# A hybrid decoder layer: the gate's row through DRAM, shift columns in the high operand alone, and the mean square of both boundaries with tokens on partitions

## The chip, the cores and the metric

The kernel runs on one core of one Trainium2 chip. The metric is the time on the device in microseconds (us), the median over timed runs. PE is TensorE's matmul stream, PEld its weight loads, DVE VectorE, ACT ScalarE, POOL GpSimd, SP the engine that issues the weight transfers.

## The reference

One decoder layer on 256 tokens of 1024 features, all in float32: a conditioning vector gives nine modulation rows; then a SwiGLU block (ffn1), a mixer of a state-space branch (SSD) and a retention branch, a second SwiGLU block (ffn2), and a last norm.

```python
def rms_normalize(x):
    return x * rsqrt(mean(x * x, axis=-1, keepdims=True) + EPS)
def modulate(x, shift, scale):
    return x * (1.0 + scale) + shift
def swiglu(x, w_in, w_out):
    gate, up = split(x @ w_in, 2, axis=-1)
    return (silu(gate) * up) @ w_out

mod = silu(c) @ ada_w + ada_b
sh1, sc1, g1, sh2, sc2, g2, sh3, sc3, g3 = split(mod, 9, axis=-1)
u = modulate(rms_normalize(h) * norm_ffn1_w, sh1, sc1)
h = h + 0.5 * g1 * swiglu(u, ffn1_w_in, ffn1_w_out)
u = modulate(rms_normalize(h) * norm_mix_w, sh2, sc2)
h = h + g2 * hybrid_mixer(u, ...)      # u @ mix_w_in, conv, SSD, retention, gates, mix_w_out
u = modulate(rms_normalize(h) * norm_ffn2_w, sh3, sc3)
h = h + 0.5 * g3 * swiglu(u, ffn2_w_in, ffn2_w_out)
return rms_normalize(h) * norm_final_w
```

## The kernel before

Activations lie transposed: features on the 128 partitions (eight tiles of 128 features, "kt" when they are contracted), the 256 tokens along the free axis. Weights come once from DRAM in tiles of 1 MB, issued on SP into four buffers (`wst`). Each tile is split in two halves, and each half in a high part (ACT, L137) and a low part (DVE, L138) of type fp32r, into four buffers `wh`; activations have a high and a low part too (`uh`, `ul`). Each product is three matmuls (mm3): high weights with `uh` (L152), high weights with `ul` (L153), low weights with `uh` (L154), 256 columns each; every fifth kt has the same three in another order (L148 to L150). Products of fp32 operands, a handful, are made by PE in several passes; the trace counts each pass.

There are two boundaries, the end of ffn1 and the end of the mixer. There `contract` finishes h feature tile by feature tile; `done` (in `residual`) scales it, adds its square to a running sum, and writes h·am, not normalised, to `ha` and `uh`/`ul`. `modulated` then runs the first four tiles of the next projection early, on this unnormalised h·am (`early_project`), because the scale 1/rms of a token can be applied to the products afterwards. The modulation's shift must not be scaled by it, so it rides along as two more columns: the moving operand is 258 columns wide, and column 256 of the product becomes a bias (`eb`). The first tiles take four PSUM banks. At kt = 1 (first boundary) or kt = 2 (second), `rstd` is called: two fp32 matmuls with a 128x128 matrix of 1/1024 sum the squares over the features and spread the result to all partitions (L223), ACT takes a logarithm and an exponential, and DVE corrects the result in four instructions (L228 to L231). `rs`, 128x256, then multiplies h·am (L274), from which the proper u is made for all later tiles (L240, L241), and the four early products (L281). `rstd` is used inside the mixer too, for its norms.

The mixer's steps run in the order of the string `ORDER`. A scheduler places each step's instructions on the engines within that order. The step "dt" projects 32 columns, turns them with an fp32 matmul (L613) and makes dt and `av` on DVE (L616 to L631); "z.0.0" is the first gate tile; "decays" makes three groups of fp32 matmuls on `av` (L684, L687, L692); "conv" steps project two tiles and run a convolution of four taps on ACT and DVE (L574, L577).

In ffn2's loop, at p2 == 5, the row 0.5·g3 (1024 values that lie on the partitions as 128x8) is made into `gb`, the same row on all 128 partitions: a diagonal matrix on DVE (L992), two fp32 matmuls with a matrix of ones (L996) and two copies on ACT (L998). `gb` is first read at the end of ffn2 (L1014), where tokens lie on the partitions.

Of the kernel before, what the change touches and what calls it, by code (L numbers as in the profile page):

```python
# [12 lines left out]
F32 = mybir.dt.float32  # L13
# [3 lines left out]
ALU = mybir.AluOpType  # L17

P = 128
# [19 lines left out]
U_ROW = 320  # L39
HALVES_AT = {"still": (6, 1056), "alike": (48, 1072)}  # L40

K_TRI, K_M = 0, 128
K_INV, K_SGN = 256, 257
N_CONST = 258

H_ID, H_N1, H_AB = KD * T, KD * T + P, KD * T + P + KD
N_HEAD = H_AB + 2 * KD
# [5 lines left out]
F1 = 8  # L53

ORDER = (
# [12 lines left out]
def constants():  # L68
    c = np.zeros((P, N_CONST), np.float32)
    i = np.arange(P)  # L70
    c[:, K_TRI:K_TRI + P] = i[:, None] <= i[None, :]
    c[:, K_M:K_M + P] = 1.0 / D
    c[:, K_INV] = 10000.0 ** (-(i % 64) / 64.0)
    c[:, K_SGN] = np.where(i < 64, -1.0, 1.0)
    lg = np.log1p(-np.exp2(-5.0 - np.arange(8)))
    rel = np.arange(T)[None, :] - i[:, None]
    dm = np.where(rel >= 0, np.exp(lg[:, None, None] * np.maximum(rel, 0)), 0.0) * P ** -0.5
    dm = np.ascontiguousarray(dm.transpose(1, 0, 2).reshape(P, 8 * T)).astype(np.float32)
    return c, dm
# [3 lines left out]
def layer(ctx: ExitStack, tc: tile.TileContext, a, out, packing):  # L83
# [72 lines left out]
    def at(pair, *idx):  # L156
        return pair[0][idx], pair[1][idx]

    def wide_at(u, kt):
        return u[2][:, kt, :], u[3][:, kt, :]  # L160

    al = slice(None)

# [2 lines left out]
    h = head[:, :KD * T].rearrange("p (f t) -> p f t", f=KD)  # L166
    ident = head[:, H_ID:H_ID + P]
    triu = k[:, K_TRI:K_TRI + P]
    mean_m = k[:, K_M:K_M + P]
    ones = cst.tile([P, P], F32, name="ones")  # L170
    dve.memset(ones, 1.0)
    epsc = cst.tile([P, 1], F32, name="epsc")
    dve.memset(epsc, EPS)

# [45 lines left out]
    def rstd(parts, mean):  # L220
        ps = misc_ps()
        for i, s in enumerate(parts):
            pe.matmul(ps[:, :T], mean, s, start=i == 0, stop=i == len(parts) - 1)  # L223
        rs = sp.tile([P, T], F32, tag="rs", name=nm("rs"), bufs=2)
        t = sp.tile([P, T], F32, tag="rt", name=nm("rt"), bufs=2)
        lookup(rs, ps[:, :T], AF.Ln, bias=epsc)
        lookup(rs, rs, AF.Exp, scale=-0.5)
        dve.tensor_tensor(t, rs, rs, ALU.mult)  # L228
        dve.scalar_tensor_tensor(t, ps[:, :T], EPS, t, ALU.add, ALU.mult)
        dve.tensor_scalar(t, t, -0.5, 1.5, ALU.mult, ALU.add)  # L230
        dve.tensor_tensor(rs, rs, t, ALU.mult)  # L231
        return rs

    def new_u():
        full = [sp.tile([P, KD, U_ROW], F32R, tag=n, name=nm(n), bufs=1) for n in ("uh", "ul")]
        return tuple(t[:, :, :T] for t in full) + tuple(t[:, :, :T + 2] for t in full)

    def u_tile(u, f, t, jsh):
        sh = modc[:, jsh, f:f + 1]
        act.activation(u[0][:, f, :], t, AF.Identity, bias=sh)  # L240
        dve.scalar_tensor_tensor(u[1][:, f, :], t, sh, u[0][:, f, :].bitcast(F32),  # L241
                                 ALU.add, ALU.subtract)
# [20 lines left out]
    ready = []  # L263

    def modulated(ha, u, jsh, w, cols, at_kt=1, c_next=None):
        rs = []
        ps = early_project(w, cols, u, at_kt, lambda: rs.append(rstd(sums, mean_m)))
        rs = rs[0]
        if c_next is not None:
            st = load(w, 0, KD, c_next, 256)  # L270
            ready.append(half(st[:, :, :P]))
        for f in range(KD):
            t = ha(f)
            dve.tensor_tensor(t, t, rs, ALU.mult)  # L274
            u_tile(u, f, t, jsh)
        if c_next is not None:
            ready.append(half(st[:, :, P:]))
        b = sp.tile([P, 4], F32, tag="eb", name=nm("eb"), bufs=1)
        for i in range(4):
            dve.tensor_copy(b[:, i:i + 1], ps[i][:, T:T + 1])  # L280
            dve.tensor_tensor(ps[i][:, :T], ps[i][:, :T], rs, ALU.mult)  # L281
        return [(ps[i][:, :T], b[:, i:i + 1]) for i in range(4)]

    def early_project(w, cols, u, at_kt, between):
        sts = [load(w, 0, KD, c0, 256) for c0 in cols]
        ps = [proj_ps().rearrange("p f t -> p (f t)") for _ in range(2)]
        ps += [misc_ps() for _ in range(2)]
        for kh in range(2):
            hv = [half(st[:, 4 * kh:4 * kh + 4, :]) for st in sts]
            for kk in range(4):  # L290
                kt = 4 * kh + kk
                if kt == at_kt:
                    between()
                for i in range(2):
                    for f in range(2):
                        mm3(ps[2 * i + f][:, :T + 2], at(hv[i], al, kk, slice(f * P, (f + 1) * P)),
                            wide_at(u, kt), kt == 0, kt == KD - 1)
        return ps

    def pair_halves(w, c0):  # L300
# [20 lines left out]
    def residual(jg, factor, am, ha, u, jsh):  # L321
        g = sp.tile([P, KD], F32, tag="g", name=nm("g"), bufs=2)
        dve.tensor_scalar(g, modc[:, jg, :], factor, None, ALU.mult)

        def shift():
            split_into(u[2][:, :, T:], u[3][:, :, T:],
                       modc[:, jsh, :].unsqueeze(2).broadcast_to([P, KD, 2]))

        def done(f, ps):
            if f == KD - 2:  # L330
                shift()
            dve.scalar_tensor_tensor(h[:, f, :], ps, g[:, f:f + 1], h[:, f, :], ALU.mult, ALU.add)
            square_add(f)
            act.activation(ha(f), h[:, f, :], AF.Copy, scale=am[:, f:f + 1])
            act.activation(u[0][:, f, :], h[:, f, :], AF.Copy, scale=am[:, f:f + 1])
            dve.tensor_tensor(u[1][:, f, :], ha(f), u[0][:, f, :].bitcast(F32), ALU.subtract)
        return done
# [17 lines left out]
    with (tc.tile_pool(name="ep", bufs=1) as ep,  # L355
# [25 lines left out]
        for kt in range(3):  # L381
            sts.append(ada01(kt))
            wst.append(w01(kt))
        mean1 = ep.tile([P, 1], F32, name="mean1")
        dve.memset(mean1, 1.0 / D)
        bn1 = ep.tile([P, KD], F32, name="bn1")
        cps, stat = [misc_ps() for _ in range(2)], misc_ps()
        for q in range(2):
# [107 lines left out]
    with tc.tile_pool(name=nm("fp"), bufs=1, reuse_waits="tile") as fp:  # L496
# [11 lines left out]
        for p2 in range(4, NF // 2):  # L508
# [5 lines left out]
            if p2 == 8:  # L514
# [21 lines left out]
                    dve.tensor_scalar(rr, rr, pi_lo, -pi_lo, ALU.min, ALU.max)  # L536
                    lookup(dst, rr, AF.Sin)
                dve.tensor_scalar(rope_s, rope_s, k[:, K_SGN:K_SGN + 1], None, ALU.mult)
        table("natural_log_exp_and_others")
        while ada_todo[0][0] in (2, 4):  # L540
            ada_next()
        am = scale_col(V_N2, 4)
# [4 lines left out]
    with tc.tile_pool(name="mx", bufs=1, reuse_waits="tile") as mx:  # L547
# [19 lines left out]
        def conv_pair(f0, dst):  # L567
            ps = pair_project(w_in, C_XS + f0 * P, u)
            t = mx.tile([P, 2, T], F32, tag="cv", name=nm("cv"), bufs=2)
            for f in range(2):  # L570
# [5 lines left out]
                for sh in (1, 2, 3):  # L576
# [3 lines left out]

        table_of = {"e": "natural_log_exp_and_others", "s": "silu_and_others",
                    "g": "sigmoid_and_others"}
        now = ["e"]

        def need(t):
            if now[0] != t:
# [366 lines left out]
        phase["uses"].append(cast)  # L953
        while ada_todo[0][0] == 7:
            ada_next()
        table("natural_log_exp_and_others")
        am = scale_col(V_N3, 7)
        hA = [slot([P, 4, T]) for _ in range(2)]

# [7 lines left out]
    with tc.tile_pool(name=nm("fp"), bufs=1, reuse_waits="tile") as fp:  # L967
# [5 lines left out]
        for p2 in range(NF // 2):  # L973
            if p2 == 0:
                s = fp.tile([P, 2, T], F32, tag="s", name=nm("s"), bufs=2)
                for f in range(2):
                    lookup(s[:, f, :], first[f][0], AF.Silu, bias=first[f][1])
                    dve.scalar_tensor_tensor(s[:, f, :], first[2 + f][0], first[2 + f][1],
                                             s[:, f, :], ALU.add, ALU.mult)
                split_into(ah[:, 0:2, :], alo[:, 0:2, :], s)  # L980
            else:
                pg = pair_project(w1, p2 * 256, u, ready if p2 == 1 else None)
                pu = pair_project(w1, FFN + p2 * 256, u)
                swiglu(fp, pg, pu, ah, alo, 2 * p2)
            ada_next()
            if p2 == 1:
                nc.sync.dma_start(wf, a["norm_final_w"].broadcast_to([P, D]))
            if p2 == 5:
                g = sp.tile([P, KD], F32, tag="g", name=nm("g"), bufs=2)
                dve.tensor_scalar(g, modc[:, 8, :], 0.5, None, ALU.mult)  # L990
                diag = fp.tile([P, KD, P], F32, tag="diag", name="diag")
                dve.tensor_tensor(diag, ident.unsqueeze(1).broadcast_to([P, KD, P]),  # L992
                                  g.unsqueeze(2).broadcast_to([P, KD, P]), ALU.mult)
                for q in range(2):
                    ps = misc_ps()
                    pe.matmul(ps, ones, diag[:, 4 * q:4 * q + 4, :].rearrange("p f t -> p (f t)"),  # L996
                              start=True, stop=True)
                    act.copy(gb[:, q * 512:(q + 1) * 512], ps)  # L998
            if p2 == 6:
                for tt in range(2):  # L1000
                    for q in range(2):
                        ps = misc_ps()
                        for f in range(4):
                            pe.transpose(ps[:, f * P:(f + 1) * P],
                                         h[:, q * 4 + f, tt * P:(tt + 1) * P], ident)
                        act.copy(hN[:, tt, q * 512:(q + 1) * 512], ps)
# [105 lines left out]
```

## Time and profile before

| | |
|---|---|
| median of 3 runs | 830.82 us (829.90 to 831.51) |
| profiled execution | 830.36 us, its span 828.3 us |
| granted TensorE clock, mean | 0.998 |
| PE busy | 816.0 us, 6610 instructions |
| DVE busy | 664.9 us, 997 instructions |
| ACT busy | 511.8 us, 731 instructions |
| POOL busy | 10.3 us, 21 instructions |

A row of a timeline has the start and the duration in us, the engine, the line, the operation, output<-inputs, the shapes and a count of instructions taken together; a bracket tells how long the engine stood idle before and what released it. A row of waits has the total in us, the number of times and the longest. A row of stretches has the bounds and the length, then busy us and (instructions) of PE, PEld, DVE, ACT and POOL, the granted clock, the DMA share and GB/s. Rows by form end in busy us and mean ns of one. Rows of the chain have start, duration and what held it.

### The profile page before, as it was taken

How to read it: one execution, taken by the hardware profiler on the slowest of the kernel's cores; microseconds unless marked ns; L12 is line 12 of the kernel's file. 1: busy time of each engine (PE TensorE's matmuls, PEld its weight loads, DVE VectorE, ACT ScalarE, POOL GpSimd, SP SyncE). 2: the span in 40 equal slices, each digit the busy share in tenths (PEclk: the TensorE clock that was granted, in tenths of full speed). 3: DMA queues.
4: the chain of work that ended last, by engine and by line, in shares of the span. 5: the costliest groups of instructions: out<-in, count | busy, mean ns of one | idle time of the engine just before them, and what ended most of it. 6: DMA issues, size and time to landing. Idle time of an engine off the chain costs nothing.

```text
span 828.3 us, 15880 instructions
## 1 busy us (share of the span) xinstructions
PE 816.0 (99%) x6610; PEld 786.7 (95%) x6610; DVE 664.9 (80%) x997; ACT 511.8 (62%) x731; POOL 10.3 (1%) x21
## 2 busy tenths in 40 slices
PE   8999999999999999999999999999999999999996
PEld 6999999999999989999999999999999999999885
DVE  6999899977989987787898778977979985455463
ACT  6565455555898787766465569765568654545442
POOL 0000000000200010000000000000000000000000
PEclk9999999999999999999999999999999999999999
DMA  9998899854695465537658754555665695455521
GB/s 361 413 419 333 317 365 350 344 180 161 238 316 190 167 216 181 196 133 237 233 184 301 253 205 153 209 199 173 219 215 183 256 345 197 169 196 183 206 77 51
DMA packets 30297, 193.06 MB, mean 233 GB/s; under 512 B 3457, under 2 KB 4097, under 8 KB 9618
## 3 DMA queue, kind: packets, MB, share of 16 engines
q1 hardware_dynamic: 28512, 186.59, 62.1%
q0 software_dynamic: 1568, 5.28, 2.0%
q8 instruction: 51, 0.84, 0.4%
q10 hardware_dynamic: 146, 0.20, 0.1%
q14 instruction: 20, 0.16, 0.1%
HBM read 190.97 MB, written 1.08 MB: 232 GB/s over the span
## 4 chain that ended last, share of the span: by engine, by line
PE 88%; DVE 4%; ACT 3%; DMA 3%; issue 1%; SPq 0%; ACTq 0%
PE proj L154 22%; PE proj L152 22%; PE proj L153 22%; PE proj L1028 7%; PE proj L148 2%; PE proj L149 2%; PE proj L150 2%; DMA wst<-in_ffn_w_in_dram 2%; ACT wh L407 1%; DMA ada<-in_ada_w_dram 1%; PE misc L757 1%; DVE wh L138 1%; PE misc L901 1%; DVE wh L410 1%; DVE ada L197 1%
## 5 line engine op out<-in xcount | busy, mean ns | idle before, releaser
L138 DVE TENSOR_TENSOR wh<-wst,wh 128x1024 fp32r<-128x1024 f32 (+1 forms) x262 | 316.7, 1212 | 110.5 <-ACT wh L137 109.8
L137 ACT CAST wh<-wst 128x1024 fp32r<-128x1024 f32 (+1 forms) x262 | 272.3, 1042 | 174.6 <-PE proj L154 104.0
L152 PE MATMUL proj<-uh,wh 128*128 128x256 f32 (+1 forms) x1144 | 317.9, 278 | 0.0
L153 PE MATMUL proj<-ul,wh 128*128 128x256 f32 (+1 forms) x1144 | 316.8, 277 | 0.5 <-DVE ul L429 0.5
L154 PE MATMUL proj<-uh,wh 128*128 128x256 f32 (+1 forms) x1144 | 316.6, 277 | 0.2 <-DVE wh L410 0.2
L153 PEld LDWEIGHTS proj<-ul,wh 128*128 128x128 f32 x1144 | 214.8, 188 | 1.2 <-DVE ul L429 0.7
L154 PEld LDWEIGHTS proj<-uh,wh 128*128 128x128 f32 x1144 | 214.8, 188 | 0.6 <-DVE wh L410 0.4
L152 PEld LDWEIGHTS proj<-uh,wh 128*128 128x128 f32 x1144 | 214.9, 188 | 0.3 <-ACT wh L137 0.2
L152 PE MATMUL proj<-s,wh 128*128 128x256 f32 x312 | 87.1, 280 | 0.2 <-ACT s L142 0.2
L154 PE MATMUL proj<-s,wh 128*128 128x256 f32 x312 | 86.4, 277 | 0.0
L153 PE MATMUL proj<-s,wh 128*128 128x256 f32 x312 | 86.2, 277 | 0.0
L152 PEld LDWEIGHTS proj<-s,wh 128*128 128x128 f32 x312 | 58.5, 188 | 0.6 <-ACT s L142 0.4
L153 PEld LDWEIGHTS proj<-s,wh 128*128 128x128 f32 x312 | 58.6, 188 | 0.2 <-issue 0.2
L154 PEld LDWEIGHTS proj<-s,wh 128*128 128x128 f32 x312 | 58.6, 188 | 0.0
L197 DVE SCALAR_TENSOR_TENSOR ada<-ada,cb 128x1024 f32<-128x1024 f32 x48 | 57.4, 1217 | 0.0
L1028 PE MATMUL proj<-wh,ah 128*128 128x512 f32 (+1 forms) x188 | 55.0, 376 | 0.5 <-DVE t L1014 0.5
L148 PE MATMUL proj<-uh,wh 128*128 128x256 f32 x152 | 42.0, 277 | 0.0
L149 PE MATMUL proj<-uh,wh 128*128 128x256 f32 x152 | 42.0, 276 | 0.0
L150 PE MATMUL proj<-ul,wh 128*128 128x256 f32 x152 | 42.0, 276 | 0.0
L153 PE MATMUL proj<-al,wh 128*128 128x256 f32 x152 | 42.0, 276 | 0.0
L152 PE MATMUL proj<-ah,wh 128*128 128x256 f32 x152 | 42.0, 276 | 0.0
L154 PE MATMUL proj<-ah,wh 128*128 128x256 f32 x152 | 42.0, 276 | 0.0
(276 smaller groups left out, 1303.2 us busy)
## 6 DMA issues: line engine op xcount, KB each, us to landing
wst<-in_mix_w_in_dram SPq DMA_DIRECT2D x52, 1024.0 KB, 4.9
wst<-in_ffn_w_in_dram SPq DMA_DIRECT2D x43, 1024.0 KB, 6.4
wst<-in_ffn_w_out_dram SPq DMA_DIRECT2D x18, 1024.0 KB, 5.1
ada<-in_ada_w_dram SPq DMA_DIRECT2D x16, 1024.0 KB, 8.4
wst<-in_ada_w_dram SPq DMA_DIRECT2D x12, 1024.0 KB, 5.0
ada<-in_ada_w_dram SPq DMA_DIRECT2D x16, 512.0 KB, 12.7
wst<-in_w_br_ssd_dram SPq DMA_DIRECT2D x8, 1024.0 KB, 4.9
wst<-in_w_br_ret_dram SPq DMA_DIRECT2D x8, 1024.0 KB, 4.9
```

The costliest lines, as they stand in the source:

```text
L137: act.copy(hi, v)
L138: dve.tensor_tensor(lo, v, hi.bitcast(F32), ALU.subtract)
L148: pe.matmul(o, l[1], r[0], start=False, stop=False, skip_group_check=skip)
L149: pe.matmul(o, l[0], r[0], start=False, stop=False, skip_group_check=skip)
L150: pe.matmul(o, l[0], r[1], start=False, stop=False, skip_group_check=skip)
L152: pe.matmul(o, l[0], r[0], start=first, stop=False, skip_group_check=skip)
L153: pe.matmul(o, l[0], r[1], start=False, stop=False, skip_group_check=skip)
L154: pe.matmul(o, l[1], r[0], start=False, stop=last, skip_group_check=skip)
L197: dve.scalar_tensor_tensor(st[:, i, :], st[:, i, :], 1.0, cb, ALU.mult, ALU.mult, accum_out=raw[:, j, f0 + i:f0 + i + 1])
L407: act.copy(hw[0][j], wst[kt][:, j, :])
L410: dve.tensor_tensor(hw[1][j], wst[kt][:, j, :], hw[0][j].bitcast(F32), ALU.subtract)
L1028: pe.matmul(ps[tt][:, part], l[:, kt, ts], r, start=kt == n == 0, stop=n == 2 and kt == NF - 1, skip_group_check=bi == 1)
```

## The change

Four things are changed.

1. The gate's row: the 128x8 tile is written to DRAM in feature order, and read back broadcast to all partitions, by two DMAs on POOL's queue. Diagonal, matmuls and copies are gone.
2. The shift columns: the high part of the shift stands in column 256 of `uh` and its low part in column 257. The middle matmul of an early product takes 256 columns of `ul`; the bias is the sum of both columns of the product (a reduction over two elements in place of a copy). The other two matmuls stay at 258.
3. The mean square at both boundaries: the sums of squares are the stationary operand and a single column of 1/1024 the moving one, two halves of 128 tokens each (`stat`), so that the mean square comes out with tokens on partitions, 128x2. The second `stat`, for the last feature's square, stands behind the first pair of tiles of that kt. A square root on ACT and a reciprocal on DVE follow on 128x2. One pair of tiles after the start of the next kt, two matmuls with r broadcast as stationary operand and the identity as moving one spread r as a 128x256 tile in PSUM (`spread`). The first four features are multiplied straight from PSUM, the others and the four early products by a copy in SBUF (`rs`). The tables loaded on ACT change to suit.
4. `ORDER` begins with "z.0.0 dt" in place of "dt z.0.0". The constant tile `k` is 128 columns narrower, since the mean matrix isn't needed, so all tiles allocated behind it lie 480 bytes lower in each partition (448 for some).

```diff
@@ constants @@
-K_TRI, K_M = 0, 128
-K_INV, K_SGN = 256, 257
-N_CONST = 258
+K_TRI, K_INV, K_SGN = 0, 128, 129
+N_CONST = 130
@@ ORDER @@
-    "dt z.0.0 decays ml.0 ml.1 conv.8 ...
+    "z.0.0 dt decays ml.0 ml.1 conv.8 ...
@@ layer @@
-    def wide_at(u, kt):
-        return u[2][:, kt, :], u[3][:, kt, :]
+    def mm3_shifted(o, l, u, kt, first, last):
+        pe.matmul(o[:, :T + 2], l[0], u[2][:, kt, :], start=first, stop=False)
+        pe.matmul(o[:, :T], l[0], u[1][:, kt, :], start=False, stop=False)
+        pe.matmul(o[:, :T + 2], l[1], u[2][:, kt, :], start=False, stop=last)
@@
-    mean_m = k[:, K_M:K_M + P]
+    mean1 = cst.tile([P, 1], F32, name="mean1")
+    dve.memset(mean1, 1.0 / D)
@@ modulated @@
-        rs = []
-        ps = early_project(w, cols, u, at_kt, lambda: rs.append(rstd(sums, mean_m)))
-        rs = rs[0]
+        work = []
+
+        def stat(i):
+            if i == 0:
+                work.append(misc_ps())
+            for tt in range(2):
+                pe.matmul(work[0][:, tt:tt + 1], sums[i][:, tt * P:(tt + 1) * P], mean1,
+                          start=i == tt == 0, stop=i == tt == 1, skip_group_check=True)
+
+        def spread():
+            r = sp.tile([P, 2], F32, tag="r2", name=nm("r2"), bufs=1)
+            lookup(r, work[0][:, :2], AF.Sqrt, bias=epsc)
+            dve.reciprocal(r, r)
+            for c in range(2):
+                pe.matmul(work[0][:, T + c * P:T + (c + 1) * P], r[:, c:c + 1].broadcast_to([P, P]),
+                          ident, start=True, stop=True)
+
+        ps = early_project(w, cols, u, {(at_kt, 0): lambda: stat(0), (at_kt, 1): lambda: stat(1),
+                                        (at_kt + 1, 1): spread})
+        spread_rs = work[0][:, T:]
+        rs = sp.tile([P, T], F32, tag="rs", name=nm("rs"), bufs=2)
...
-            dve.tensor_tensor(t, t, rs, ALU.mult)
+            dve.tensor_tensor(t, t, spread_rs if f < 4 else rs, ALU.mult)
             u_tile(u, f, t, jsh)
+            if f == 1:
+                act.copy(rs, spread_rs)
...
-            dve.tensor_copy(b[:, i:i + 1], ps[i][:, T:T + 1])
+            dve.tensor_reduce(b[:, i:i + 1], ps[i][:, T:T + 2], mybir.AxisListType.X, ALU.add)
@@ early_project @@
-                if kt == at_kt:
-                    between()
                 for i in range(2):
+                    if (kt, i) in steps:
+                        steps[kt, i]()
                     for f in range(2):
-                        mm3(ps[2 * i + f][:, :T + 2], at(hv[i], al, kk, slice(f * P, (f + 1) * P)),
-                            wide_at(u, kt), kt == 0, kt == KD - 1)
+                        mm3_shifted(ps[2 * i + f], at(hv[i], al, kk, slice(f * P, (f + 1) * P)),
+                                    u, kt, kt == 0, kt == KD - 1)
@@ residual @@
-            split_into(u[2][:, :, T:], u[3][:, :, T:],
-                       modc[:, jsh, :].unsqueeze(2).broadcast_to([P, KD, 2]))
+            split_into(u[2][:, :, T], u[2][:, :, T + 1], modc[:, jsh, :])
@@ before the mixer, and before the second boundary @@
-        table("natural_log_exp_and_others")
+        table("sqrt_and_others")
@@
-        now = ["e"]
+        now = ["q"]
@@ ffn2, p2 == 5 @@
-                diag = fp.tile([P, KD, P], F32, tag="diag", name="diag")
-                dve.tensor_tensor(diag, ident.unsqueeze(1).broadcast_to([P, KD, P]),
-                                  g.unsqueeze(2).broadcast_to([P, KD, P]), ALU.mult)
-                for q in range(2):
-                    ps = misc_ps()
-                    pe.matmul(ps, ones, diag[:, 4 * q:4 * q + 4, :].rearrange("p f t -> p (f t)"),
-                              start=True, stop=True)
-                    act.copy(gb[:, q * 512:(q + 1) * 512], ps)
+                grow = dp.tile([1, KD, P], F32, name="grow")
+                nc.gpsimd.dma_start(grow.rearrange("o f p -> p (o f)"), g)
+                nc.gpsimd.dma_start(gb.rearrange("p (f q) -> p f q", f=KD),
+                                    grow.broadcast_to([P, KD, P]))
```

On PE at the first boundary, before (L152 to L154 are the three matmuls of an early product, L223 the mean square; a number behind a name is the buffer):

```order
L154 MATMUL misc_2345<-uh_140,wh_2349 128x258
L223 MATMUL misc_2364<-ssum_1762,k 128x256
L223 MATMUL misc_2364<-sq_2333,k 128x256
L152 MATMUL proj_2342<-uh_140,wh_2346 128x258
L153 MATMUL proj_2342<-ul_141,wh_2346 128x258
```

And now (L158 to L160 are the three matmuls, L273 `stat`):

```order
L160 MATMUL misc_2345<-uh_140,wh_2349 128x258
L273 MATMUL misc_2364<-mean_80,ssum_1762 128x1 x2
L158 MATMUL proj_2342<-uh_140,wh_2346 128x258
L159 MATMUL proj_2342<-ul_141,wh_2346 128x256
L160 MATMUL proj_2342<-uh_140,wh_2346 128x258
L158 MATMUL proj_2343<-uh_140,wh_2346 128x258
L159 MATMUL proj_2343<-ul_141,wh_2346 128x256
L160 MATMUL proj_2343<-uh_140,wh_2346 128x258
L273 MATMUL misc_2364<-mean_80,sq_2333 128x1 x2
```

The first group stands where the old two calls stood, the second six matmuls later; the spread (L281) follows twelve matmuls behind that. On DVE in the mixer's first steps, before (L625 to L631 are the end of dt, L138 a weight half, L577 a tap of the convolution):

```order
L625 TENSOR_SCALAR m_2534<-m_2534 128x64
L627 SCALAR_TENSOR_TENSOR m_2534<-m_2534 128x64 x7
L628 SCALAR_TENSOR_TENSOR m_2534<-m_2534 128x64
L630 SCALAR_TENSOR_TENSOR dt_2505<-m_2534 128x64
L138 TENSOR_TENSOR wh_2735<-wst_2732,wh_2735 128x1024
L631 SCALAR_TENSOR_TENSOR av_2506<-dt_2505,m_2534 128x64
L577 SCALAR_TENSOR_TENSOR cv_2654<-proj_2599,col,cv_2654 128x255
```

And now the end of it (L645 to L649 are L627 to L631 of before, L136 a weight half, L595 a tap):

```order
L645 SCALAR_TENSOR_TENSOR m_2542<-m_2542 128x64
L595 SCALAR_TENSOR_TENSOR cv_2723<-proj_2668,col,cv_2723 128x255
L646 SCALAR_TENSOR_TENSOR m_2542<-m_2542 128x64
L595 SCALAR_TENSOR_TENSOR cv_2723<-proj_2668,col,cv_2723 128x254
L648 SCALAR_TENSOR_TENSOR dt_2506<-m_2542 128x64
L595 SCALAR_TENSOR_TENSOR cv_2723<-proj_2668,col,cv_2723 128x253
L649 SCALAR_TENSOR_TENSOR av_2507<-dt_2506,m_2542 128x64
```

The taps of two products of conv.8 now stand between dt's instructions, where they stood behind `av`; on PE L613 (now L631) comes ten matmuls later, and the decays' matmuls some 53 rows later.

More of the change, by code (lines that the diff above doesn't have):

```diff
@@ L71, in constants @@
     c[:, K_TRI:K_TRI + P] = i[:, None] <= i[None, :]
-    c[:, K_M:K_M + P] = 1.0 / D
     c[:, K_INV] = 10000.0 ** (-(i % 64) / 64.0)
@@ L235, in new_u @@
         full = [sp.tile([P, KD, U_ROW], F32R, tag=n, name=nm(n), bufs=1) for n in ("uh", "ul")]
-        return tuple(t[:, :, :T] for t in full) + tuple(t[:, :, :T + 2] for t in full)
+        return tuple(t[:, :, :T] for t in full) + (full[0][:, :, :T + 2],)
     def u_tile(u, f, t, jsh):
@@ L279, in modulated, with early_project @@
         for i in range(4):
-            dve.tensor_copy(b[:, i:i + 1], ps[i][:, T:T + 1])
+            dve.tensor_reduce(b[:, i:i + 1], ps[i][:, T:T + 2], mybir.AxisListType.X, ALU.add)
             dve.tensor_tensor(ps[i][:, :T], ps[i][:, :T], rs, ALU.mult)
         return [(ps[i][:, :T], b[:, i:i + 1]) for i in range(4)]
-    def early_project(w, cols, u, at_kt, between):
+    def early_project(w, cols, u, steps):
         sts = [load(w, 0, KD, c0, 256) for c0 in cols]
@@ L383, in layer @@
             wst.append(w01(kt))
-        mean1 = ep.tile([P, 1], F32, name="mean1")
-        dve.memset(mean1, 1.0 / D)
         bn1 = ep.tile([P, KD], F32, name="bn1")
@@ L955, in layer @@
             ada_next()
-        table("natural_log_exp_and_others")
+        table("sqrt_and_others")
         am = scale_col(V_N3, 7)
```

2 rows, old and new, of the table ORDER are left out of this document.

## The prediction

> **What bounds the kernel now.** I read the page first, then the list of PE's waits, then a table of stretches, and last the instructions at the places that the change touches.
>
> ```profile
> span 828.3 us, 15880 instructions
> PE 816.0 (99%) x6610; PEld 786.7 (95%) x6610; DVE 664.9 (80%) x997; ACT 511.8 (62%) x731; POOL 10.3 (1%) x21
> q0 software_dynamic: 1568, 5.28, 2.0%
> PE 88%; DVE 4%; ACT 3%; DMA 3%; issue 1%; SPq 0%; ACTq 0%
> ```
>
> PE is busy 99% of the span and holds 88% of the chain that ended last. The third row, POOL's DMA queue, is used further down. What PE waits for:
>
> ```profile
> PE misc L389 <- DMA crow<-in_c_dram: 3.1, 1, 3.1
> PE misc L901 <- DVE m L892: 0.6, 1, 0.6
> ```
>
> After the start-up the largest entry is one wait of 0.6 us. And in ffn1:
>
> ```profile
> 54.00:192.60 138.60, 138.60 (x1224) 138.60 (x1225) 122.05 (x183) 73.90 (x97) 0.00 (x0) 1.00 0.83 315
> ```
>
> 1224 matmuls in 138.60 us at a granted clock of 1.00: one starts every 113 ns, without a gap. So the change is worth what it takes out of PE's stream, less what it puts in; ACT and DVE instructions count only where PE comes to wait for them. Durations in the rows overlap (a matmul of 256 columns lasts 0.28 us and the next starts 0.113 us later), so I price by start times.
>
> **Mean square, what goes.** The two calls of L223 at each boundary:
>
> ```profile
> 195.82 0.28 PE L154 MATMUL misc<-uh,wh 128*128 128x258 f32 x1
> 195.94 0.60 PE L223 MATMUL misc<-ssum,k 128*128 128x256 f32 x2
> 196.55 0.70 PE L223 MATMUL misc<-sq,k 128*128 128x256 f32 x2
> 196.90 0.47 PE L152 MATMUL proj<-uh,wh 128*128 128x258 f32 x1
> 197.21 0.29 PE L153 MATMUL proj<-ul,wh 128*128 128x258 f32 x1
> ...
> 638.77 0.28 PE L154 MATMUL misc<-uh,wh 128*128 128x258 f32 x1
> 639.56 0.47 PE L152 MATMUL proj<-uh,wh 128*128 128x258 f32 x1
> 639.88 0.28 PE L153 MATMUL proj<-ul,wh 128*128 128x258 f32 x1
> ```
>
> From the last matmul before to the second one behind: 197.21 − 195.82 = 1.39 us at the first boundary, 639.88 − 638.77 = 1.11 at the second. Two matmuls at 0.12 would have taken 0.24, so L223 costs 1.15 and 0.87, **2.02 us** together. The first is dearer by a wait for the last square (0.42 us on the weights' side):
>
> ```profile
> 196.55 0.30 PEld L223 LDWEIGHTS misc<-sq,k 128*128 128x128 f32 x2 [0.42 <-ACT sq L252]
> ```
>
> The change reads that square six matmuls (0.7 us) later, so the wait goes with the price.
>
> **Mean square, what comes.** Each fp32 call is two passes, as L223's x2 shows. At each boundary there are two groups of two calls with one column (four passes each) and one group of two calls with 128 columns (four passes, the spread). The trace has no one-column call in a full-speed stretch. The nearest rows:
>
> ```profile
> 209.30 0.28 PE L152 MATMUL proj<-uh,wh 128*128 128x256 f32 x1
> 209.62 0.52 PEld L613 LDWEIGHTS misc<-m,m 64*128 64x128 f32 x4 [0.25 <-ACT m L610]
> 210.40 0.28 PE L154 MATMUL proj<-uh,wh 128*128 128x256 f32 x1
> ...
> 277.63 1.79 PE misc L672 x16
> 292.08 1.95 PE misc L757 x32
> ...
> 6.80 0.93 PEld L397 LDWEIGHTS misc<-mean,sq 128*128 128x128 f32 x4 [1.50 <-ACT cb L186]
> 9.02 1.40 PEld L378 LDWEIGHTS misc<-ones 128*128 128x128 f32 x6
> ```
>
> L613 is four passes of 32 columns between ordinary matmuls. 210.40 − 209.30 = 1.10, less two matmuls (0.23) and 0.21 of waiting (209.62 against 209.41) leaves 0.67 us for the group. L672 makes passes of 128 columns in 1.79/16 = 0.112 us, and L757, with half the weights, in 1.95/32 = 0.061. At the start, where everything runs at about half pace, L397 is one-column: 0.93/4 = 0.23 us a pass, beside 1.40/6 = 0.23 with 128 columns. So the pass is set by the weights that it loads, not by its columns, and a one-column group should cost about what L613 does: I take 0.64 (four passes of 0.112 and the 0.19 that L613 shows beyond them), with 0.45 (four passes alone) and 0.67 as bounds. The spread is 4 x 0.112 = 0.45, and with L613's entry and exit 0.64. Per boundary 2 x 0.64 + 0.45 = 1.73 (1.35 to 1.98), both **3.46 us** (2.70 to 3.96). Net of the 2.02 removed: **+1.44** (+0.68 to +1.94).
>
> In the Trainium skill, "TensorE: Matmul & The Clock Gate", section "LDWEIGHTS (loading the stationary operand)", a load costs its columns over 1.2 ns, 107 ns for 128; L672's 112 agrees, and the sum would be the same. The same page's section "Wait — 56ns, not 53.3ns?" has a floor of about 25 ns from start to start however few the columns; no row of this case shows it.
>
> **What waits for the mean.** Before, the chain began with a logarithm (ACT, L186) and the first multiply by the scale started at 199.95 (DVE, L274):
>
> ```profile
> 197.29 0.48 ACT L186 ACTIVATE rs<-misc,epsc 128x256 f32<-128x256 f32 x1
> 199.95 1.10 DVE L274 TENSOR_TENSOR nT<-nT,rs 128x256 f32<-128x256 f32 x3
> ...
> 9.26 0.26 ACT L186 ACTIVATE r<-misc,epsc 128x2 f32<-128x2 f32 x1 [0.45 <-PE misc L397]
> 9.56 0.17 DVE L457 RECIPROCAL r<-r 128x2 f32<-128x2 f32 x1 [0.24 <-ACT r L186]
> ```
>
> The new chain has its short form at the start-up: a [128x2] square root 0.26, a reciprocal 0.17. The second group ends near 195.94 + 0.64 + 0.72 + 0.64 = 197.9, the root and reciprocal are done by 198.5, and PE comes to the spread twelve matmuls (1.4 us) after the second group, at 199.3. PE does not wait, and the multiply starts at about 199.9, where it did. Six wide ACT and DVE instructions on DVE's chain become two tiny ones and one copy of 128x256 behind the second feature; that is free here, because PE has seven kt steps of early products left at L223 (84 matmuls at 0.12, 10 us) and needs the new u only behind them. If PE did wait at the spread, every matmul of the early tiles would queue behind it: the margin is 0.8 us.
>
> **Gate's row.**
>
> ```profile
> 702.86 0.28 PE L154 MATMUL proj<-uh,wh 128*128 128x256 f32 x1
> 702.98 1.88 PE L996 MATMUL misc<-diag,ones 128*128 128x512 f32 x4
> 704.81 0.28 PE L153 MATMUL proj<-ul,wh 128*128 128x256 f32 x1
> ...
> 676.33 0.17 DVE L990 TENSOR_SCALAR g<-modc 128x8 f32<-128x8 f32 x1
> 790.65 1.28 DVE L1014 TENSOR_TENSOR t<-proj,gb 128x512 f32<-128x512 f32 x2
> 676.00:680.00 4.00, 4.00 (x38) 4.00 (x37) 3.01 (x6) 2.56 (x3) 0.00 (x0) 1.00 0.91 297
> 681.41 1.05 ACT L137 CAST wh<-wst 128x1024 fp32r<-128x1024 f32 x1 [1.62 <-PE proj L154]
> ```
>
> 704.81 − 702.86 = 1.95, less two matmuls (0.23): **−1.72 us**, certain, since nothing on PE takes its place. The diagonal on DVE and two copies on ACT go too, off the path. What comes are two DMAs on POOL's queue, which is idle there. The first writes 1024 elements of four bytes. At the queue's mean, 2.0% of 16 x 828.3 us over 1568 packets, one packet is 0.17 us of an engine, so 1024 over 16 engines take some 11 us (an estimate, from packets of 3.4 KB), and the second 512 KB. The row is needed at 790.65, 114 us after g: its latency is hidden. SP's weight loads share the engines at 676 to 680, where they are 91% busy; but at 681.41 ACT waits for PE to free a half, not for a load, so loads are ahead of use there. In the Trainium skill, "DMA: Bandwidth & Descriptors", section "Rules for kernel authors", a strided last dimension becomes one descriptor per element and is to be avoided: that speaks against the edit; by it the write is those 1024 packets, and the sum stays.
>
> **Narrow middle matmul.** 64 of them lose two columns.
>
> ```profile
> L153 PE MATMUL proj<-ul,wh 128*128 128x258 f32 x32 | 9.0, 282 | 0.0
> L153 PE MATMUL proj<-ul,wh 128*128 128x256 f32 x1112 | 307.8, 277 | 0.5 <-DVE ul L429 0.5
> ```
>
> 5 ns at most, 64 x 5 = 0.32; at least nothing, if the wide neighbours set the pace. I take **−0.2**. The reduction that sums the two columns replaces a copy of one column on DVE.
>
> **Order.** "dt" behind "z.0.0" puts L613 ten matmuls (1.1 us) later and the decays some 53 (6.0 us).
>
> ```profile
> 217.85 0.52 PEld L684 LDWEIGHTS misc<-av,k 128*128 128x128 f32 x4 [0.29 <-DVE av L631]
> ...
> 211.56 0.19 DVE L621 TENSOR_SCALAR m<-m 128x64 f32<-128x64 f32 x1
> 217.58 0.22 DVE L631 SCALAR_TENSOR_TENSOR av<-dt,m 128x64 f32<-128x64 f32 x1
> 217.72 0.47 DVE L577 SCALAR_TENSOR_TENSOR cv<-proj,col,cv 128x255 f32<-128x255 f32 x1
> ```
>
> Gain: both waits, 0.21 and about 0.25, go. Loss: DVE's work from L621 to L631 (6 us now) gets nine convolution taps of 0.47 woven in and a half of 1.2 more, and starts 1.1 later: 4.2 + 1.2 + 1.1 = 6.5 against the 6.0 that the decays moved, so av is later by 0.5 and the wait up to 0.9 (the conv products queue behind it on PE). I take 0, with −0.46 to +0.7.
>
> **Sum.** 1.44 − 1.72 − 0.2 + 0 = −0.48. From the profiled execution's 830.36 (2.06 around the span) 829.9; that execution lies 0.46 below the median of the runs, 830.82, so **830.3** on the median. Bounds: 0.68 − 1.72 − 0.32 − 0.46 = −1.8 and 1.94 − 1.72 + 0 + 0.7 = +0.9: 829.0 to 831.7.
>
> **Rivals.** (a) One-column passes are nearly free, their weights being loaded while the wide matmul before them runs. For: L757's 0.061 us with half the weights. Against: L613 with 32 columns pays in full. At 0.061 the two groups and the spread are 12 x 0.061 = 0.73 a boundary, 1.46 in both, net −0.56, and with the rest −2.5: 828.3, faster. The 25 ns floor that the skill's page states would make it a little more.
> (b) Slower: the layout. The constant tile shrinks by 512 bytes per partition, and every tile behind it (weights, halves, u, activations) moves; relative places of the operands change. The price is taken from the 5 ns by which a matmul of the 258-column form is longer. Were a third of the matmuls of that commonest form (three lines of 1112) put there, it is 1112 x 0.005 = +5.6, and 835.9. It decides from some 430 matmuls on (2.1 us). For: the source keeps hand-set offsets for the halves, so spacing depends on places. Against: halves and u move together.
> (c) The decays' wait takes the place of the gain, +0.7 and no part of the −0.2: 831.2, still the same.
> (d) Slower: the 1024 small packets delay weight loads. 11 us of each engine, in a stretch 91% busy, could set loads back some 7 us; what the loads' lead doesn't cover of that, PE waits for. The lead is not in one row; with half of it uncovered, +3.5: 833.8. It decides from 2.2 us uncovered.
> (e) The boundary chain is later than I worked out and PE waits at the spread, 0.5 to 1 us each time: +1.5, 831.8, the edge of the same.
>
> **Chances.** About 0.2% (1.7 us) is what a measurement of this kernel can tell from no change: 829.2 and 832.5. My sum 0.57; (a) 0.16; (b) 0.06; (c) 0.11; (d) 0.04; (e) 0.06. Faster: (a) and a tail 0.02 of the sum, 0.18. Slower: (b), (d) and 0.02 of (e), 0.12. Same: 0.70. The range leaves out (b), (d) and half of (a), and takes in the rest: 828.6 to 832.2.
>
> **What would show it.** At each boundary the two one-column groups and the spread: about 0.64, 0.64, 0.45 from the starts of the matmuls around them; under 0.3 says (a). No L996 near 703, and no PE wait for g's row at 790. The row of waits: L613's gone, the decays' between 0 and 0.9. In ffn1's stretch 113 ns a matmul; 118 there, or in the branches, says (b). PE waiting for a weight half between 676 and 720 says (d). I am wrong if the passes' price is off by more than half, or if some stretch that the edits do not touch changes its pace.

## The result, and the profile after

The changed kernel takes 839.75 us (839.20 to 840.33, 4 runs) against 830.53 for the kernel before in the same runs (829.90 to 831.51): a ratio of 1.0113, interval 1.0102 to 1.0125. It is 9.2 us slower; 830.3 was forecast, with a range of 828.6 to 832.2.

The page of the changed kernel (span, busy time by engine, POOL's queue with packets, MB and share):

```profile
span 837.4 us, 15900 instructions
PE 824.5 (98%) x6622; PEld 794.7 (95%) x6622; DVE 661.1 (79%) x990; ACT 510.2 (61%) x729; POOL 11.7 (1%) x23
q0 software_dynamic: 1744, 5.81, 2.2%
```

PE is busy 8.5 us more with 12 more instructions. So the time is on PE, and the few new instructions don't hold it. The same stretch of 50 us in ffn1's second half, first of the kernel before, then of the changed one (bounds, length, busy us and instructions of PE, PEld, DVE, ACT and POOL, granted clock, DMA share, GB/s):

```profile
140.00:190.00 50.00, 50.00 (x444) 50.00 (x443) 40.14 (x62) 26.29 (x39) 0.00 (x0) 1.00 0.72 266
```

```profile
140.00:190.00 50.00, 50.00 (x427) 50.00 (x426) 39.07 (x61) 25.94 (x39) 0.00 (x0) 1.00 0.67 252
```

No edit touches this stretch, PE has no gap in it, the clock is 1.00 in both, and PE starts 427 matmuls where it started 444: 117.1 ns from one to the next, not 112.6. Which matmuls are slow is told by the rows by form (busy us, mean ns), before:

```profile
L152 PE MATMUL proj<-s,wh 128*128 128x256 f32 x312 | 87.1, 280 | 0.2 <-ACT s L142 0.2
L152 PE MATMUL proj<-ah,wh 128*128 128x256 f32 x152 | 42.0, 276 | 0.0
L1028 PE MATMUL proj<-wh,ah 128*128 128x512 f32 x164 | 50.5, 389 | 0.0
```

and after, the same lines with their new numbers:

```profile
L150 PE MATMUL proj<-uh,wh 128*128 128x256 f32 x1112 | 308.2, 277 | 0.0
L150 PE MATMUL proj<-s,wh 128*128 128x256 f32 x312 | 88.5, 284 | 0.1
L152 PE MATMUL proj<-ah,wh 128*128 128x256 f32 x152 | 42.8, 281 | 0.0
L1042 PE MATMUL proj<-wh,ah 128*128 128x512 f32 x164 | 51.5, 396 | 0.0
```

Matmuls on `uh` keep their 277 ns. Those on `ah` and `al` (the high and low part of a SwiGLU's silu(gate)·up) and on `s` (the mixer's activations) are 4 to 5 ns longer, and the 512-column ones at the end of ffn2, where `ah` and `al` are the stationary operand, 7 ns. There are 1488 with 256 columns: 3 x 312 on `s`, 3 x 152 on `ah` and `al`, and 96 in the other order of the three matmuls. The 246 with 512 columns stand together on the chain (start, duration), before:

```profile
761.17 55.80 PE proj L1028 x246
```

and after:

```profile
768.73 57.42 PE proj L1042 x246
```

These are 1.6 us longer. If each of the 1488 starts 117.1 − 112.6 = 4.5 ns later than it did, they add 6.7: some 8.3 us in all, an estimate that takes ffn1's 4.5 ns for `s` too.

Second, where the changed kernel falls behind, by the start of the same instruction before and after:

| place | before | after | lag |
|---|---|---|---|
| last early product ahead of the first mean square | 195.82 | 197.84 | +2.0 |
| transposes of "bc" (L672, now L690) | 277.46 | 280.66 | +3.2 |
| first state product (L757, now L775) | 292.01 | 295.23 | +3.2 |
| first matmul of L152, now L150, behind L767, now L785 | 294.87 | 299.64 | +4.8 |
| last early product ahead of the second mean square | 638.77 | 647.55 | +8.8 |
| transposes behind the gate's row (L1004, now L1018) | 715.71 | 723.26 | +7.6 |
| end of the span | 828.3 | 837.4 | +9.1 |

The stretches between hold slow matmuls, apart from two. From 198 to 299 no matmul of weights with `ah`, `al` or `s` runs, and still the lag grows by 2.8 us, 1.2 of it ahead of "bc" and 1.6 at the state products. Between the second boundary and 716 the kernel gains. At the state products PE's waits have an entry that was not there:

```profile
PE misc L785 <- ACT st L737: 1.4, 1, 1.4
```

Behind it stands ACT. POOL's and ACT's rows of the timeline before (start, duration, idle before and its releaser):

```profile
222.19 1.13 POOL L727 DMA_DIRECT2D m<-rows  x2 [1.52 <-DMA rows<-m]
...
227.69 0.69 ACT L738 ACTIVATE m<-m,cs 128x128 f32<-128x128 f32 x2 [1.09 <-DMA m<-rows]
```

and after, with DVE's:

```profile
227.79 0.67 POOL L713 DMA_DIRECT2D rows<-m  x1 [227.35 <-DVE dend L706]
233.25 1.10 POOL L745 DMA_DIRECT2D m<-rows  x2 [4.79 <-DMA rows<-m]
...
238.82 0.40 ACT L756 ACTIVATE m<-m,cs 128x128 f32<-128x128 f32 x1 [4.96 <-DMA m<-rows]
...
239.71 2.63 DVE L595 SCALAR_TENSOR_TENSOR cv<-proj,col,cv 128x255 f32<-128x255 f32 x5 [4.59 <-ACT cv L592]
```

The decays' rows go to DRAM and come back as masks, and the masks' first activation on ACT waits for them: 1.09 us before, 4.96 after. The convolutions' activations and the weight halves are queued behind it, and DVE behind these.

### The profile page after: what moved, and what is told of

Read it like the earlier page. It is cut to its first block, busy times and chain, and to the rows that moved or that the text cites. A ratio compares the mean times of both kernels' runs of the same rounds, so it can differ in the third digit from the quotient of the medians.

```text
span 837.4 us, 15900 instructions
## 1 busy us (share of the span) xinstructions
PE 824.5 (98%) x6622; PEld 794.7 (95%) x6622; DVE 661.1 (79%) x990; ACT 510.2 (61%) x729; POOL 11.7 (1%) x23
## 3 DMA queue, kind: packets, MB, share of 16 engines
q0 software_dynamic: 1744, 5.81, 2.2%
HBM read 191.43 MB, written 1.09 MB: 230 GB/s over the span
## 4 chain that ended last, share of the span: by engine, by line
PE 60%; issue 29%; ACT 5%; DVE 4%; DMA 1%; ACTq 0%; POOL 0%; POOLq 0%
PE proj L152 15%; PE proj L150 15%; PE proj L151 15%; PE proj L1042 7%; DVE cv L595 1%; PE proj L146 1%; PE proj L148 1%; PE proj L147 1%; ACT m L756 1%; DVE wh L136 1%; ACT s L187 1%; ACT wh L135 1%; PE misc L919 1%; PE misc L775 1%; DMA m<-rows 1%
## 5 line engine op out<-in xcount | busy, mean ns | idle before, releaser
L136 DVE TENSOR_TENSOR wh<-wst,wh 128x1024 fp32r<-128x1024 f32 (+1 forms) x262 | 317.0, 1213 | 114.9 <-ACT wh L135 114.3
L152 PE MATMUL proj<-uh,wh 128*128 128x256 f32 x1112 | 307.9, 277 | 0.5 <-DVE wh L428 0.2
L150 PE MATMUL proj<-uh,wh 128*128 128x256 f32 x1112 | 308.2, 277 | 0.0
L151 PE MATMUL proj<-ul,wh 128*128 128x256 f32 x1112 | 307.3, 276 | 0.0
L152 PEld LDWEIGHTS proj<-uh,wh 128*128 128x128 f32 x1112 | 208.6, 188 | 1.5 <-DVE wh L136 0.9
L150 PEld LDWEIGHTS proj<-uh,wh 128*128 128x128 f32 x1112 | 208.8, 188 | 0.2 <-ACT wh L135 0.2
L151 PEld LDWEIGHTS proj<-ul,wh 128*128 128x128 f32 x1112 | 208.8, 188 | 0.0
L150 PE MATMUL proj<-s,wh 128*128 128x256 f32 x312 | 88.5, 284 | 0.1
L152 PE MATMUL proj<-s,wh 128*128 128x256 f32 x312 | 87.8, 282 | 0.0
L151 PE MATMUL proj<-s,wh 128*128 128x256 f32 x312 | 87.7, 281 | 0.0
L150 PEld LDWEIGHTS proj<-s,wh 128*128 128x128 f32 x312 | 59.0, 189 | 0.5 <-ACT s L140 0.3
L152 PEld LDWEIGHTS proj<-s,wh 128*128 128x128 f32 x312 | 58.7, 188 | 0.0
L152 PE MATMUL proj<-ah,wh 128*128 128x256 f32 x152 | 42.8, 281 | 0.0
L150 PE MATMUL proj<-ah,wh 128*128 128x256 f32 x152 | 42.7, 281 | 0.0
L1042 PEld LDWEIGHTS proj<-wh,ah 128*128 128x128 f32 x188 | 34.5, 188 | 8.1 <-DVE t L1028 0.7
L146 PE MATMUL proj<-uh,wh 128*128 128x256 f32 x152 | 42.1, 277 | 0.0
L148 PE MATMUL proj<-ul,wh 128*128 128x256 f32 x152 | 42.0, 276 | 0.0
```

The lines of the kernel that those rows point to most:

```text
L136: dve.tensor_tensor(lo, v, hi.bitcast(F32), ALU.subtract)
L146: pe.matmul(o, l[1], r[0], start=False, stop=False, skip_group_check=skip)
L148: pe.matmul(o, l[0], r[1], start=False, stop=False, skip_group_check=skip)
L150: pe.matmul(o, l[0], r[0], start=first, stop=False, skip_group_check=skip)
L151: pe.matmul(o, l[0], r[1], start=False, stop=False, skip_group_check=skip)
L152: pe.matmul(o, l[1], r[0], start=False, stop=last, skip_group_check=skip)
```

## The experiments

Three questions: what slowed the matmuls on `ah` and `s`, what the order costs, and what each of the other edits is worth alone. In the built programs, the first buffer `wh` and `ah` (and the first `s`) lay 61632 bytes apart in each partition before, and 61664 after. `uh` and `ul` lie between the two, and behind them now `r2`, the 128x2 tile of the new mean square, whose 8 bytes a partition take up 32. The four buffers `wh` follow each other at 8448 = 33 x 256 bytes.

**r2_cst**: the changed kernel with that one tile elsewhere.

```diff
-            r = sp.tile([P, 2], F32, tag="r2", name=nm("r2"), bufs=1)
+            r = cst.tile([P, 2], F32, tag="r2", name=nm("r2"), bufs=1)
```

> The changed kernel with its one new small tile r (two columns) allocated in the pool of constants ahead of the weight tiles, and not between the weight halves and the activations; nothing else differs. Theory A (layout): r's 32 bytes moved ah, al and s by 32 bytes relative to the weight halves, and each of their matmuls went from 113 to 118 ns; restored, 113 everywhere and 839.75 - 8 = 831.8 us. Rival B (absolute places: ah and s lie 448 bytes lower in each partition than before, and here still do): no change, 839.8, 118 ns stay.

Measured: 831.48 us (830.67 to 833.54), ratio to before 1.0014 (1.0004 to 1.0023). 8.3 of the 9.2 us are gone. The form by its row:

```profile
L150 PE MATMUL proj<-s,wh 128*128 128x256 f32 x312 | 87.1, 280 | 0.2 <-ACT s L140 0.2
```

87.1 us and 280 ns, as before. `ah` and `s` lie where they lay in the changed kernel, and only the halves lie 32 bytes higher, so rival B falls.

**pad_s32**: the kernel before, with 32 unused bytes.

```diff
         u = new_u()
+        sp.tile([P, 8], F32, tag="pad", name="pad", bufs=1)
```

> The kernel before with an unused tile of 32 bytes per partition allocated behind uh and ul, so that ah, al, s and all that follows them lie 32 bytes further from the weight halves; no instruction differs. Theory A: ah, al and s matmuls at 118 ns, uh and ul at 113: about +8 us, 838.5. Rival B, or a cost that lies in the new instructions: no change, 830.5.

Measured: 837.84 us, ratio 1.0090 (1.0074 to 1.0105): 7.7 us for a tile that nothing uses.

```profile
L152 PE MATMUL proj<-s,wh 128*128 128x256 f32 x312 | 88.5, 284 | 0.1
```

284 ns again, as in the changed kernel, with every instruction as before. Here the halves lie where they did and `ah` and `s` 32 bytes higher; in r2_cst it was the other way round. What the two runs share is the distance.

**order_back** and **both_back**: the changed kernel, and r2_cst, with the old beginning of the order.

```diff
-    "z.0.0 dt decays ml.0 ml.1 conv.8 ...
+    "dt z.0.0 decays ml.0 ml.1 conv.8 ...
```

> The changed kernel with dt ahead of z.0.0 again. Theory O: with the decays 53 rows later the rows' trip through DRAM ended later (4.8 us against 1.5 of waiting on POOL), ACT stood idle 5.0 us for the masks, and PE paid 1.4 us at one matmul on st and some 1.5 us in the convolutions: -2.9, 836.9. Rival: that stall was made up on PE and the order is worth nothing, 839.8, or the old waits at dt and the decays come back, 840.2.

> The changed kernel with r in the pool of constants and dt ahead of z.0.0. Theories A and O together: 839.75 - 8 - 2.9 = 828.9 us, faster than before by about 1.6. If something of the mean square, the gate or the narrow matmul costs that I have not seen, it shows here: 830.5 or more.

Measured: order_back 836.67 us, 3.1 less than the changed kernel; both_back 828.65 (828.36 to 829.46), 2.8 less than r2_cst, and 0.9983 (0.9973 to 0.9992) of before. So the order costs 3.1 us with the slow distance and 2.8 without it, and the distance 8.3 with the new order and 8.0 (836.67 − 828.65) with the old: neither cause needs the other. In both runs the wait at L785 is gone. The rest of the order's cost lies in the convolutions (stretches as above). order_back:

```profile
245.00:270.00 25.00, 25.00 (x223) 25.00 (x222) 22.79 (x37) 21.82 (x43) 0.00 (x0) 1.00 0.60 209
```

The changed kernel:

```profile
245.00:270.00 25.00, 24.82 (x211) 24.23 (x210) 22.17 (x37) 24.12 (x55) 0.00 (x0) 1.00 0.66 221
```

12 matmuls fewer, at 0.112 us each, are 1.3 us; with 1.6 at the state products that is 2.9 of the 3.1. With layout and order undone, what remains of the change is 1.5 us faster than the kernel before.

**late_masks**: how the order costs it. r2_cst, with dt still second, but the masks' activations held behind the fourth convolution's Silu.

```diff
             lookup(dst, t, AF.Silu)
+            silus.append(phase["uses"][-1])
...
-                act.activation(m[c][:, hl, :], m[c][:, hl, :], AF.Relu,
-                               bias=cs[:, c, hd:hd + 1], scale=-1.0)
+                with tc.issue_after(silus[3]):
+                    act.activation(m[c][:, hl, :], m[c][:, hl, :], AF.Relu,
+                                   bias=cs[:, c, hd:hd + 1], scale=-1.0)
```

> r2_cst (the changed kernel with r among the constants) with the masks' first activations on ACT placed behind the fourth convolution's Silu; dt still behind z.0.0, PE's, DVE's and POOL's order as in r2_cst. Theory O1: the decays' lateness costs time only because ACT stands in order at the first mask (5.0 us in the changed kernel, 6.5 in r2_cst) with weight halves and convolutions queued behind it; then the wait goes, PE's 1.4 us at st too, and 831.5 - 2.8 = 828.7. Theory O2: the masks themselves, or the decays on PE, are late for what needs them; then 831.5 stays.

Measured: 828.92 us (828.28 to 829.29), 2.6 less than r2_cst. The masks' first activation now finds its rows there:

```profile
240.38 0.63 ACT L187 ACTIVATE s<-cv 128x512 f32<-128x512 f32 x1
240.91 1.27 ACT L760 ACTIVATE m<-m,cs 128x128 f32<-128x128 f32 x4
```

It starts later than in r2_cst (238.65) and costs nothing; L785's wait is gone. So the lateness of the decays was no cost in itself (theory O2 falls): the cost was ACT standing in order at the masks. Why the rows were late beyond the decays' own 5.6 us is in the rows of the transfer (KB each, median us from issue to landing) and the stretch in which it was issued. both_back:

```profile
220.00:222.00 2.00, 2.00 (x20) 2.00 (x19) 2.00 (x4) 1.79 (x3) 0.67 (x1) 1.00 0.07 16
...
rows<-m POOLq DMA_DIRECT2D x1, 32.0 KB, 1.9
```

r2_cst:

```profile
226.00:228.00 2.00, 2.00 (x19) 2.00 (x19) 1.97 (x4) 1.97 (x3) 0.67 (x1) 1.00 0.76 262
...
rows<-m POOLq DMA_DIRECT2D x1, 32.0 KB, 5.5
```

The same 32 KB landed in 1.9 us with the DMA engines 7% busy, and in 5.5 with 76%, with DVE as busy in both (2.00 and 1.97 us of 2). The traced execution of r2_cst, 833.54 us, is the slowest of its ten; in the changed kernel's trace the same transfer took 5.2. That the weight loads were the reason fits, but the load was not varied by itself, so it is argued, not shown.

**gate_only**, **gate_narrow**, **mean_only**: the kernel before with one or two edits of the change (mean_only with `r2` among the constants), all with the layout distance and order of before; their diffs are those of the change.

> The kernel before with the gate's row through DRAM alone. My sum: -1.72 for the two matmuls on PE and some -0.1 for the slower matmuls behind them: 830.2 - 1.8 = 828.4. Rival (the 1024 small packets hold back weight loads): 830 or more.

> The kernel before with the gate's row through DRAM and the shift columns in the high operand alone; mean square, order and layout of before. My sum: -1.8 and -0.2 (the trace of both_back, 347 ns for three matmuls against 355, says up to -0.5): 828.2 to 827.9, faster than both_back's 828.65. If the narrow matmul is worth nothing: as gate_only, 828.4.

> The kernel before with the new mean square alone, r among the constants; gate, shift columns and order of before. By the forecast's prices +1.44: 831.6. By the traces of after and both_back (three groups of 0.44 a boundary = 2.66 in all, against 2.02 removed) +0.64, and +0.4 if PE's wait for a weight half at 655 belongs to it: 830.8 to 831.2. Rival (one-column passes nearly free): 829.6.

Measured: gate_only 828.49 us (827.71 to 828.99), 0.9975 (0.9964 to 0.9985) of before. gate_narrow 828.56, 0.9978 (0.9968 to 0.9987). mean_only 830.38, 1.0000 (0.9991 to 1.0009). So the gate's row is worth 1.7 us, the narrow matmul nothing that can be measured, and the mean square 0.2 us with an interval of some 0.8 either way, which leaves out the forecast's +1.44. gate_only, the smallest edit, is the fastest of all kernels here, but by less than its interval from both_back, both_pad256, gate_narrow and late_masks.

**pad_s64**, **pad_s96**, **pad_s128**, **pad_all32**, **both_pad256**: which distances are slow. The pad of pad_s32 with other sizes; in pad_all32 it is allocated ahead of `uh` and `ul`; in both_pad256 it is added to both_back.

> The kernel before with an unused tile of 64 bytes per partition behind uh and ul (pad_s32 had 32 and took 837.8). If what counts is the place of the activations relative to the weight halves in a period of 64 bytes: 113 ns again, 830.2. If any distance other than that of before is slow: 837.8.

> The same with 96 bytes. Period of 64 bytes: as with 32, 118 ns for ah, al and s, 837.8. Otherwise 830.2.

> The kernel before with the unused 32 bytes allocated ahead of uh and ul, so that these too lie 32 bytes further from the weight halves. If the relative place is the cause for every moving operand, uh's and ul's matmuls (some 4000 of 256 columns) go to 118 ns too: 20 us beside the 7.6 of pad_s32, 858. If only ah, al and s are touched: 837.8.

> The kernel before with an unused tile of 128 bytes per partition behind uh and ul (32, 64 and 96 bytes took 837.8, 839.2 and 839.8). If the distance to the weight halves counts in a period of 128 bytes: 113 ns for ah, al and s, 830.2. If only the exact distance of before is fast, or the period is longer: 838 to 840.

> both_back (the changed kernel with r among the constants and dt first; 828.65) with an unused tile of 256 bytes behind uh and ul. Of the distances tried so far, 32, 64, 96 and 128 bytes more are slow. If the period is 256 bytes: 113 ns for ah, al and s, 828.7. If only the exact distance of before is fast, or the period is longer: 836 to 838.

| kernel | bytes added to the distance of before | us |
|---|---|---|
| before | 0 | 830.2 to 830.7 |
| pad_s32 | 32 | 837.84 |
| pad_s64 | 64 | 839.16 |
| pad_s96 | 96 | 839.81 |
| pad_s128 | 128 | 837.34 |
| both_back | 0 | 828.65 |
| both_pad256 | 256 | 828.56 |
| pad_all32 | 32, for `uh` and `ul` too | 853.78 |

My periods of 64 and of 128 bytes both fell: four distances are slow, by 6.6 to 9.6 us, and 256 more bytes are as good as none. A period of 256 fits all of them, but it rests on one fast distance besides that of before; 160, 192 and 224 weren't tried. pad_all32 shows that `uh` and `ul` obey the same rule:

```profile
L152 PE MATMUL proj<-uh,wh 128*128 128x256 f32 x1112 | 313.6, 282 | 0.0
```

282 ns in place of 277; 23.5 us in all, where I expected 28. In the kernel before both distances from the start of a buffer `wh`, 33984 bytes to `uh` and 61632 to `ah`, leave 192 when divided by 256; the changed kernel kept the first and moved the second to 224. The 192 itself is a matter of this kernel: in its buffer, the high part of a half starts at byte 24 and the low part at byte 4224 for these matmuls (`HALVES_AT`), so the operands' own distances to `ah` leave 168 and 64, and both are fast.

## Why the prediction was wrong

**The total held within its bounds where the sum looked, but two costs that it put at nothing decided.** The sum said −0.48, with −1.8 and +0.9 as bounds. With layout and order undone (both_back) the change gives −1.5. The 9.2 us are the layout, 8.3 (r2_cst), and the order, 2.8 (both_back), less that 1.5. The 0.4 that this is too much is the kernel before, whose median was 830.53 beside the changed kernel and 830.18 beside these runs.

**The layout** was rival (b), at 0.06. Its mechanism was right, and its sign was seen: 117.1 ns a matmul in ffn1. Its price of 5 ns was near (276 to 281 ns), but by luck, since it was taken from matmuls with two more columns, which have nothing to do with places. It said +5.6 by a third of the matmuls on `uh`, and the measured 8.3 come from others, 1488 on `ah`, `al` and `s` and 246 of 512 columns. The step that failed is the argument against it: "halves and u move together". They do, by 480 bytes; `ah`, `al` and `s` moved by 448, which stood in the description of the change and was not weighed. Where the source itself sets the places of the halves by hand, a difference of 32 bytes between two operands of some 1500 matmuls deserved more than 6%.

**The order** was taken as 0, between −0.46 and +0.7, and costs about 2.9. I followed DVE's work up to `av` and stopped at PE's matmuls on it. Neither of the two waits that I priced decides: the decays' matmuls have no wait of 0.2 us or more in the list after, and the one for `m` stays:

```profile
PEld misc L631 <- ACT m L628: 0.3, 1, 0.3
```

What I left out is the next link: the decays' rows go through DRAM on POOL's queue to the masks, and ACT stands at these with 1.09 us of idle time already in the trace before. With that row I had the waiting instruction, and did not ask what is queued behind it. Rival (c) named the right step and the wrong wait.

**The mean square** was priced at +1.44 (+0.68 to +1.94). The first boundary after:

```profile
197.84 0.28 PE L160 MATMUL misc<-uh,wh 128*128 128x258 f32 x1
197.95 0.50 PE L273 MATMUL misc<-mean,ssum 128*128 128x1 f32 x4
198.31 0.36 PE L158 MATMUL proj<-uh,wh 128*128 128x258 f32 x1
198.52 0.29 PE L159 MATMUL proj<-ul,wh 128*128 128x256 f32 x1
...
200.88 0.28 PE L160 MATMUL proj<-uh,wh 128*128 128x258 f32 x1
201.00 0.60 PE L281 MATMUL misc<-head,r 128*128 128x128 f32 x4
201.36 0.36 PE L158 MATMUL misc<-uh,wh 128*128 128x258 f32 x1
201.56 0.28 PE L159 MATMUL misc<-ul,wh 128*128 128x256 f32 x1
```

A group of four one-column passes: 198.52 − 197.84 = 0.68, less two matmuls (0.24), 0.44 us; the spread 201.56 − 200.88 − 0.24 = 0.44. So a pass costs 0.11 with 1 column as with 128, as I worked out, and rival (a) falls. In the Trainium skill, "TensorE: Matmul & The Clock Gate", section "LDWEIGHTS (loading the stationary operand)", a load costs its columns over 1.2 ns, 107 ns for 128; the measured 0.11 us agrees. In the same page of the Trainium skill, section "Wait — 56ns, not 53.3ns?", the time from start to start has a floor of about 25 ns; these passes stay far above it, and no run here shows it. Mis-sized was the 0.19 for entering and leaving a group, taken from L613, whose weights have 64 rows: here it is nothing, and why L613 pays it no run tells. (Its rows give 1.10 − 0.23 − 0.21 = 0.66 for the group, so 0.21 beyond the passes; the difference is of no weight.) Three groups of 0.44 at two boundaries are 2.64, not 3.46, and net of the 2.02 removed +0.62, below my lower bound of +0.68; mean_only measures +0.2 with an interval that holds it. PE did not wait at the spread, as forecast, so rival (e) falls.

**The gate's row** was priced at −1.72; gate_only measures −1.7. Of rival (d): no PE wait shows at 680 to 760 in the changed kernel, but the collision is there. The transfers issued from 675 to 700 (KB each, median us to landing), before:

```profile
wst<-in_ffn_w_in_dram SPq DMA_DIRECT2D x5, 1024.0 KB, 6.0
```

and in gate_only, which runs in step with it there:

```profile
wst<-in_ffn_w_in_dram SPq DMA_DIRECT2D x5, 1024.0 KB, 11.1
gb<-grow POOLq DMA_DIRECT2D x1, 512.0 KB, 8.2
grow<-g POOLq DMA_DIRECT2D x1, 4.0 KB, 11.5
```

Weight loads landed 5 us later, and their lead hid it: gate_only has no new PE wait there either. The 1024 elements are not 1024 packets: POOL's queue has 1744 − 1568 = 176 more in all, for the write and the broadcast of 512 KB together. So the estimate of 11 us on each engine came from a wrong count, and still the write of 4 KB took 11.5 us to land. In the Trainium skill, "DMA: Bandwidth & Descriptors", section "Rules for kernel authors", a transfer with a strided last dimension, as this write has in DRAM, becomes one descriptor per element; the trace does not count descriptors.

**The narrow matmul**, −0.2 with 0 and −0.32 as bounds: gate_narrow is 0.07 us above gate_only, within the noise. Not told apart from nothing.

## What to carry to other kernels

A change that adds or removes an on-chip tile, however small, moves every tile allocated behind it: before pricing its instructions, compare the distances between the operands of the commonest matmuls before and after, and keep them, with a tile's size or its pool (32 bytes cost 8 us here, 1%). When a step is moved, follow its results past the next engine to the first instruction that waits for them in order, a transfer through DRAM included, and count what is queued there. A pass of PE with a single moving column was no cheaper here than one with 128 (0.11 us), while L223's four passes of 256 columns cost 0.87, 0.22 each: up to 128 columns, fp32 reductions here are priced by passes, not by columns.

## What the runs showed of the hardware that was not expected

The time of a 256-column matmul depends on the distance in SBUF between the stationary and the moving operand: 113 ns from start to start at the distance of before, 117 to 118 at 32, 64, 96 and 128 bytes more, 113 again at 256 bytes more (both_pad256 beside both_back), with the same instructions in each pair, PE busy throughout the stretch of ffn1 from which the times are taken (444 matmuls in 50 us against 423 to 428), and a granted clock of 0.997 to 0.999 in all. It holds for `uh`, `ul`, `ah`, `al` and `s` as moving operands, and for `ah` and `al` as the stationary one with 512 moving columns of weights (389 to 396 ns a matmul). What in the memory does it was not tried, nor whether the absolute places matter beside the distance; in r2_cst the halves and all these activations lie 448 bytes lower than before, at the same speed.
